# A two-layer diffusion step on one core: the modulation in 12 units of 1024 columns instead of 48 of 256

## The chip, the core and the metric

The kernel runs on one core of a Trainium2 chip. That core has TensorE (PE, with its weight loads as PEld), VectorE (DVE), ScalarE (ACT), GpSimd (POOL), SyncE (SP, which issues nearly all weight loads) and 16 DMA engines. The metric is the device time of one execution in microseconds (us), the median of three runs.

## The reference, cut to what matters

Each of two layers makes six vectors per condition from a small product, the modulation, and uses them around two halves of the layer (token mixer and expert retrieval).

```
adaLN: (shift1, scale1, gate1, shift2, scale2, gate2) = split(SiLU(cond) @ w_mod + b_mod)
h = LN(x) * (1 + scale1) + shift1        -> one projection h @ w_in, three mixers, merge
x = LN(alpha * x + gate1 * mix)
PEER (expert retrieval) on LN(x) * (1 + scale2) + shift2
x = LN(alpha * x + gate2 * ffn)
```

D_MODEL is 1024, so w_mod is 1024 x 6144 for each layer: 24 MB a layer in float32. There are two conditions only (`c_ctx` for 128 context tokens, `c` for 256 latent tokens), so the product has two rows. Its result is wanted by channel: channel on the partition, one column for each condition.

## The kernel before, in words

The 384 tokens are three tiles of 128. `mcol` holds the modulation by channel: [128 partitions, layer, part 0 to 5, 8 groups of 128 channels, 2 conditions]. Parts 0, 1 and 2 (shift1, scale1, gate1) are wanted around the mixer, 3, 4 and 5 around PEER.

A unit (`adaln_unit`) makes 256 of the 6144 columns of a layer. It loads two tiles of 512 KB (`load_k`), each with four of the eight 128-row slices of w_mod. Eight matmuls with a stationary operand of 32 columns (`condT`, two of them live) and 256 moving columns go to the four 32-wide column groups of TensorE: slice k goes to group k % 4, so four run side by side, and two are added in each group (L259). ScalarE copies the sums to `modp` (L261). Later two matmuls with the constant `sel` add the four groups and turn the result to channels (L265), and two ScalarE operations add the bias into `mcol` (L268). There are 24 units a layer, 48 in all. `adaln` begins a unit and finishes the one begun before it, so the turning of a unit stands one unit behind its product.

Where the 48 units stand: 8 in the start stage, between the transposes of the first LayerNorm (L441), for parts 0 and 1 of layer 0; 16 between the blocks of the `w_in` projection of layer 0, one after every second block (`blocks`); 4 at the entry to PEER of layer 0 and 10 in `tick`, one for each query block from the sixth on; 8 between the `w_in` blocks of layer 1 and 2 at the entry to its PEER.

A `w_in` block (`proj3`) is a load of 512 KB, a ScalarE cast to a high part (L222, `uh`), a subtraction for the low part (L224, `ul`; on GpSimd for the first three blocks, then on VectorE) and 24 matmul rows of 384 columns (L368 to L370).

Every weight load, of w_mod too, takes one of eight buffers `w` (`N_RAW`) and is issued by SP in the order written. A load waits until the buffer that it takes has been read. A scheduler chooses the order of each engine's instructions within what the data allow; PSUM buffers are rings of two to three by tag (`pp`, `pt`, `pa`; in PEER `uT` with one and `hp` with three).

The conditioning and bias are loaded by rows and turned to channels with one and two TensorE transposes (`cond_prep`).

Of the kernel before, what the change touches and what calls it, by code (L numbers as in the profile page):

```python
# [14 lines left out]
AF = mybir.ActivationFunctionType  # L15
# [22 lines left out]
N_PRE = (14, 18)  # L38
N_EXP = (10, 16)
P_TAIL = 5  # L40
N_FILL = (16, 8)
N_AD = (4, 4)
N_END = 0
N_AFF = 640
P_AFF = 512
# [5 lines left out]
N_GS = 0  # L51
U_R = {}
N_PSC = 8
R_AD = 4
CE_G = 0
S_NORM = 512
MOD_V = 1
# [50 lines left out]
    return t  # L108


CAND = []
_o = 0
for _i in range(8):
# [42 lines left out]
def hybrid_step(ctx: ExitStack, tc: tile.TileContext, A, O):  # L156
# [16 lines left out]
    def mk(p, shape, tag, dt=F32, bufs=None):  # L173
        uid[0] += 1
        kw = {} if bufs is None else {"bufs": bufs}
        return p.tile(shape, dt, name=f"{tag}_{uid[0]}", tag=tag, **kw)
# [48 lines left out]
        return hi, lo  # L225

    spool = [None]
    fill_ps, fill_n, first = [None], [0], [0]


    def cond_prep(sp, ps1):
        cond = mk(sp, [16, 128], "cond")
        dma(out=cond[0:8, :], in_=A["c_ctx"].rearrange("(k p) -> k p", p=128))
        dma(out=cond[8:16, :], in_=A["c"].rearrange("o (k p) -> (o k) p", p=128))
        V.memset(condT, 0.0)
        ps = mk(ps1, [128, 512], "pt")
        T.transpose(ps[:, :16], cond, ident[:16, :16])
        th = mk(sp, [128, 16], "cth")
        S.activation(th, ps[:, :16], AF.Tanh, scale=0.5)
        cc = mk(sp, [128, 16], "cc")  # L240
        S.activation(cc, ps[:, :16], AF.Copy, scale=0.5)
        V.scalar_tensor_tensor(condT[:, :, 0:2].rearrange("p k c -> p c k"), th.rearrange("p (c k) -> p c k", c=2), 1.0,
                               cc.rearrange("p (c k) -> p c k", c=2), op0=ALU.add, op1=ALU.mult)
        for l in range(DEPTH):
            bm = mk(sp, [48, 128], "bm", bufs=2)
            dma(out=bm, in_=A["b_mod"][l].rearrange("(k p) -> k p", p=128))
            ps = mk(ps1, [128, 512], "pt")
            T.transpose(ps[:, :48], bm, ident[:48, :48])
            V.tensor_copy(bmT[:, l], ps[:, :48])
            for part in (1, 4):  # L250
                V.tensor_scalar(bmT[:, l, part * KD:(part + 1) * KD], bmT[:, l, part * KD:(part + 1) * KD], 1.0, None, op0=ALU.add)

    def adaln_unit(l, part, hb, ps1, tags):

        w = load_k(A["w_mod"][l, part * 4 + hb])
        ps = mk(ps1, [128, 512], tags[0])
        for k in range(KD):
            q = k % 4
            T.matmul(ps[32 * q:32 * q + 32, :256], condT[:, k, :], w[k], start=(k < 4), stop=(k >= 4), tile_position=(0, 32 * q))  # L259
        mp = mk(outer, [128, 256], "modp", bufs=2)  # L260
        S.copy(mp, ps[:, :256])  # L261
        yield
        pt = mk(ps1, [128, 512], tags[1])
        for a in range(2):
            T.matmul(pt[:, 2 * a:2 * a + 2], mp[:, a * 128:(a + 1) * 128], sel, start=True, stop=True)  # L265
        c = part * KD + 2 * hb
        for a in range(2):
            S.activation(mcol[:, l, part, 2 * hb + a, :], pt[:, 2 * a:2 * a + 2], AF.Identity, bias=bmT[:, l, c + a:c + a + 1])  # L268

    todo = []  # L270
    for l, ps in ((0, (0, 1)), (0, (2,)), (0, (3, 4)), (1, (0, 1)), (0, (5,)), (1, (2,)), (1, (3, 4)), (1, (5,))):
        todo += [(l, part, hb) for hb in range(4) for part in ps]
    begun = []

    def adaln(n, ps1, tags, flush=False):

        for _ in range(min(n, len(todo))):
            u = adaln_unit(*todo.pop(0), ps1, tags)
            next(u)
            begun.append(u)  # L280
            if len(begun) > 1:
                next(begun.pop(0), None)
        while flush and begun:
            next(begun.pop(0), None)
# [88 lines left out]
    def blocks(src, b0, n):  # L373

        for j in range(n):
            yield load_w(src[b0 + j])
            if j % 2 and fill_n[0] > 0:
                fill_n[0] -= 1
                adaln(1, fill_ps[0], ("pp", "pt"))

# [37 lines left out]
    def mixer(l, stack, right, ps1):  # L418
# [4 lines left out]
        with ExitStack() as sc0:  # L423
            sp = pool(sc0, "ln")
            if l == 0:
                cond_prep(sp, ps1)
            hh = mk(mh, [128, KD, NTOK], "hh", dt=F32R)
            hl = mk(mh, [128, KD, NTOK], "hl", dt=F32R)

            if l == 0:  # L430

                xn = []
                for t in range(3):
                    xn.append(mk(sp, [128, D], "xn", bufs=3))
                    ln_norm(t, sp, xn[t])
                for k in range(KD):
                    if k % 2 == 0:
                        adaln(2, ps1, ("pp", "pt"), True)
                    ps = mk(ps1, [128, 512], "pa")
                    for t in range(3):  # L440
                        T.transpose(ps[:, t * 128:(t + 1) * 128], xn[t][:, k * 128:(k + 1) * 128], ident)  # L441
                    raw = mk(sp, [128, NTOK], "hraw", bufs=2)
                    for j, c in enumerate((slice(0, NP), slice(NP, NTOK))):
                        S.activation(raw[:, c], ps[:, c], AF.Identity, bias=mcol[:, l, 0, k, j:j + 1], scale=mcol[:, l, 1, k, j:j + 1])
                    parts(raw, hh[:, k, :], hl[:, k, :])
            for t in range(3 if l > 0 else 0):
                raw = mk(sp, [128, KD, 128], "hraw", bufs=2)
                ts = slice(t * 128, (t + 1) * 128)
                ln_mod_T(l, t, 0, 1, sp, mk(sp, [128, D], "xn", bufs=3), ps1, "pt", raw, lambda ks: parts(raw[:, ks], hh[:, ks, ts], hl[:, ks, ts], V if t == 2 else G))
        fill_ps[0], fill_n[0], first[0] = ps1, N_FILL[l], N_FIRST  # L450

        ysT = [mk(mo, [128, 4, NTOK], f"y{i}", dt=F32 if i else F32R) for i in range(3)]
        yl0 = mk(mo, [128, 4, NTOK], "ya", dt=F32R)
# [565 lines left out]
    def peer(l, mg, right, mps, ps1):  # L1019
# [161 lines left out]

        def tick(b):
            u_steps(U_R.get(b, 0))
            if l == 0 and b >= N_WQ + R_AD:
                adaln(1, pu, ("uT", "hp"), b == 15)
        later.append(tick)
        next(finding)
# [121 lines left out]
def blocked(inputs):  # L1309

    d = {k: np.asarray(v) for k, v in inputs.items()}

    def cut(w, k, n):

        m = w.shape[:-2]
        w = w.reshape(*m, -1, k, 128, w.shape[-1] // n, n)
        i = len(m)
        w = w.transpose(*range(i), i + 3, i, i + 2, i + 1, i + 4)
        return w.reshape(*m, w.shape[i], w.shape[i + 1], 128, k * n)

    wi = d.pop("w_in")
    d["w_in"] = cut(np.concatenate([wi[:, :, :1280], wi[:, :, 1296:]], axis=2), KD, 128)[:, :, 0]
    d["w_dt"] = cut(wi[:, :, 1280:1296], KD, 16)[:, 0, 0]
    d["peer_wq"] = cut(d["peer_wq"], KD, 128)[:, :, 0]
    d["w_mod"] = cut(d["w_mod"], 4, 256)
    d["w_out"] = cut(d["w_out"], 4, 256)
    d["w_branch"] = cut(d["w_branch"], 4, 256)[:, :, :, 0]
    return d
# [21 lines left out]
```

## Time and profile before

| | |
|---|---|
| median of three runs | 3023.25 us (3023.19 to 3025.1) |
| profiled execution, and its span | 3023.89 us, 3021.8 us |
| PE busy | 2880.1 us, 95% of the span |
| DVE, ACT, POOL busy | 77%, 46%, 27% |
| bytes moved | 767.09 MB, mean 254 GB/s |
| w_mod loads | 96 of 512 KB, median 4.4 us from issue to landing |
| w_in loads | 104 of 512 KB, median 3.7 us |

Stages on the clock of the trace: start (first LayerNorm, 8 units) to about 51 us; mixer of layer 0 to about 545 us; entry to PEER, query blocks and their ticks to 681 us; expert products and retrieval to about 1570 us; then layer 1 in the same order, with its entry to PEER at 2047 us.

The "PE busy" of the page counts an engine that has matmuls in its pipe. It is no measure of the array's pace: TensorE's granted clock is 2.4 GHz or 1.2 GHz, and a row of 384 columns follows the last by 0.17 or 0.32 us accordingly.

### The profile page before, as it was taken

To read this page: it belongs to the slowest core of one execution; us is meant where nothing else is said; L and a number is where in the kernel's file an instruction comes from. 1 tells how busy PE (TensorE), PEld (TensorE's weight loads), DVE (VectorE), ACT (ScalarE), POOL (GpSimd) and SP (SyncE) were. 2 spreads that over 40 slices of the span, in tenths; PEclk is the share of its full clock that TensorE was granted. 3 is DMA by queue.
4 is the path that set the end of the run, shared out by engine and by line. 5 is a ranking of instruction groups with operands and counts; after the bars stand their busy time and mean duration, and the time that the engine had idled before them with its cause. 6 is when DMAs were issued, how large, how long until landed. Compare 5 with 4: busy or idle time off the path is not lost. (4 is left out here: it accounts for less than half of the span.)

```text
span 3021.8 us, 48665 instructions
## 1 busy us (share of the span) xinstructions
PE 2880.1 (95%) x17953; PEld 2496.8 (83%) x17953; DVE 2314.3 (77%) x4888; ACT 1398.6 (46%) x2861; POOL 820.5 (27%) x566
## 2 busy tenths in 40 slices
PE   7999999999889999999969999999987999999996
PEld 5888889878779999998858888898876899999985
DVE  3745554599669999998977456446996999999988
ACT  4544542324864444444445445432168444444443
POOL 0000000101334445554530000000023444455554
PEclk9999999999999999999979999999999999999998
DMA  7445322464999999999934332124469999999994
GB/s 245 156 152 153 84 65 90 154 227 146 334 343 418 393 388 396 396 390 369 385 100 153 119 96 76 64 91 133 154 212 366 412 395 392 396 394 392 395 365 166
DMA packets 299328, 767.09 MB, mean 254 GB/s; under 512 B 42770, under 2 KB 113874, under 8 KB 299090
## 3 DMA queue, kind: packets, MB, share of 16 engines
q1 hardware_dynamic: 225362, 495.51, 46.0%
q0 software_dynamic: 73728, 268.47, 23.4%
q8 instruction: 141, 2.31, 0.3%
q14 instruction: 97, 0.79, 0.1%
HBM read 726.92 MB, written 36.96 MB: 253 GB/s over the span
## 5 line engine op out<-in xcount | busy, mean ns | idle before, releaser
L1052 POOL DMA_INDIRECT prow<-in_peer_u,ei x256 | 361.5, 1412 | 765.2 <-DVE prow L1057 521.6
L1063 POOL DMA_INDIRECT prow<-in_peer_v,ei x256 | 379.8, 1483 | 352.4 <-DVE tn L1068 310.8
L222 ACT CAST vh<-w 128x1024 fp32r<-128x1024 f32 x256 | 268.8, 1050 | 367.2 <-issue 285.6
L1162 PE MATMUL hp<-hh,uh 128*128 128x256 f32 x1488 | 433.8, 292 | 0.0
L1163 PE MATMUL hp<-hl,uh 128*128 128x256 f32 x1488 | 417.2, 280 | 0.0
L1164 PE MATMUL hp<-hh,ul 128*128 128x256 f32 x1488 | 416.8, 280 | 0.0
L1240 PE MATMUL out<-vh,al 128*128 128x512 f32 x1024 | 400.4, 393 | 3.6 <-DVE al L1225 3.6
L1239 PE MATMUL out<-vl,ah 128*128 128x512 f32 x1024 | 398.4, 391 | 3.1 <-DVE vl L224 3.1
L1238 PE MATMUL out<-vh,ah 128*128 128x512 f32 x1024 | 391.0, 398 | 1.4 <-ACT ah L1223 1.4
L224 DVE TENSOR_TENSOR vl<-w,vh 128x1024 fp32r<-128x1024 f32 x256 | 315.5, 1232 | 62.0 <-ACT vh L222 61.3
L1068 DVE SCALAR_TENSOR_TENSOR tn<-prow,pact,tn 128x1024 f32<-128x1024 f32 x254 | 325.0, 1280 | 2.7
L1150 ACT CAST uh<-w 128x1024 fp32r<-128x1024 f32 x186 | 195.4, 1051 | 251.7 <-PE hp L1163 243.0
L368 PE MATMUL pp<-hh,uh 128*128 128x384 f32 (+1 forms) x848 | 300.1, 354 | 8.9 <-ACT uh L222 4.7
L1057 DVE SCALAR_TENSOR_TENSOR prow<-prow,tn 128x1024 f32<-128x1024 f32 x256 | 302.2, 1218 | 0.3 <-DMA prow<-in_peer_u,ei 0.3
L370 PE MATMUL pp<-hh,ul 128*128 128x384 f32 (+1 forms) x848 | 296.3, 349 | 1.4 <-POOL ul L224 1.4
L1159 PE MATMUL hp<-hs,w 128*128 128x256 f32 x1120 | 266.5, 394 | 30.7 <-DMA w<-in_peer_uT 30.7
L369 PE MATMUL pp<-hl,uh 128*128 128x384 f32 (+1 forms) x848 | 295.0, 348 | 0.2 <-DVE xr L494 0.2
L1162 PEld LDWEIGHTS hp<-hh,uh 128*128 128x128 f32 x1488 | 281.3, 189 | 0.0
L1163 PEld LDWEIGHTS hp<-hl,uh 128*128 128x128 f32 x1488 | 281.2, 189 | 0.0
L1164 PEld LDWEIGHTS hp<-hh,ul 128*128 128x128 f32 x1488 | 280.4, 188 | 0.0
L1159 PEld LDWEIGHTS hp<-hs,w 128*128 128x128 f32 x1120 | 216.1, 197 | 63.0 <-DMA w<-in_peer_uT 33.5
L351 POOL TENSOR_TENSOR res<-res,lg 128x384 f32<-128x384 f32 x6 | 9.6, 1594 | 939.7 <-ACT res L313 939.7
(405 smaller groups left out, 5843.0 us busy)
## 6 DMA issues: line engine op xcount, KB each, us to landing
w<-in_peer_uT SPq DMA_DIRECT2D x256, 512.0 KB, 6.9
w<-in_peer_v SPq DMA_DIRECT2D x256, 512.0 KB, 7.2
w<-in_w_in SPq DMA_DIRECT2D x104, 512.0 KB, 3.7
w<-in_w_mod SPq DMA_DIRECT2D x96, 512.0 KB, 4.4
gd<-w SPq DMA_DIRECT2D x64, 512.0 KB, 6.1
gt<-gd SPq DMA_DIRECT2D x64, 512.0 KB, 7.4
w<-in_peer_wq SPq DMA_DIRECT2D x32, 512.0 KB, 4.4
w<-in_w_branch SPq DMA_DIRECT2D x24, 512.0 KB, 3.7
```

What stands on the lines that cost most here:

```text
L224: e.tensor_tensor(lo, src, hi.bitcast(F32), op=ALU.subtract)
L1052: G.indirect_dma_start(out=row, out_offset=None, in_=utab, in_offset=bass.IndirectOffsetOnAxis(ap=ei[:, j:j + 1], axis=0))
L1057: V.scalar_tensor_tensor(row, row, 1.0, tn, op0=ALU.mult, op1=ALU.mult, accum_out=hd[:, j:j + 1])
L1063: G.indirect_dma_start(out=row, out_offset=None, in_=vtab, in_offset=bass.IndirectOffsetOnAxis(ap=ei[:, j:j + 1], axis=0))
L1068: V.scalar_tensor_tensor(acc, row, act[:, j:j + 1], acc, op0=ALU.mult, op1=ALU.add)
L1159: T.matmul(o, ut[0][:, k, :], hs[:, k, :], start=(k == 0), stop=(k == KD - 1))
L1162: T.matmul(o, uh[:, k, :], hh[:, k, :], start=(k == 0), stop=False)
L1163: T.matmul(o, uh[:, k, :], hl[:, k, :], start=False, stop=False)
L1164: T.matmul(o, ul[:, k, :], hh[:, k, :], start=False, stop=(k == KD - 1))
L1238: T.matmul(o, ah[:, ts], vh[:, ns], start=f, stop=False)
L1239: T.matmul(o, ah[:, ts], vl[:, ns], start=False, stop=False)
L1240: T.matmul(o, al[:, ts], vh[:, ns], start=False, stop=e)
```

## The change

A unit now makes 1024 columns. The 48 units become 12 (`UNITS`: two for layer 0's shift1 and scale1, half of each in either, then one for each of the other ten parts). A unit loads eight tiles of 512 KB; tile k holds slice k of all 1024 columns. For each tile four matmuls run side by side, column group q taking 256 of the 1024 columns, and each group adds over all eight k. One ScalarE copy of 128 x 256 follows, two TensorE transposes of 128 x 128 (L262 of the changed kernel) and two VectorE additions with the bias, straight into `mcol` (four for the first two units). The bytes, the 96 loads and the 384 matmuls of w_mod are as many as before; 96 `sel` matmuls become 24 transposes, 48 copies become 12, 96 ScalarE additions become 28 on VectorE.

Where they stand: two in the start stage, five between the `w_in` blocks of layer 0 (after every sixth), one at the entry to PEER, three in the ticks of query blocks 9, 12 and 15, and the last between the blocks of layer 1. Conditioning and bias come from the host by channel, in two loads without transposes.

```diff
-N_FILL = (16, 8)
-N_AD = (4, 4)
+N_FILL = (5, 2)
+FILL_BY = 6
+N_AD = (1, 1)
...
+UNITS = [((0, 0, 0, 4), (0, 1, 0, 4)), ((0, 0, 4, 4), (0, 1, 4, 4))]
+UNITS += [((l, part, 0, 8),) for l, part in ((0, 2), (0, 3), (0, 4), (1, 0), (1, 1), (0, 5), (1, 2), (1, 3), (1, 4), (1, 5))]
...
     def cond_prep(sp, ps1):
-        cond = mk(sp, [16, 128], "cond")
-        dma(out=cond[0:8, :], in_=A["c_ctx"].rearrange("(k p) -> k p", p=128))
-        dma(out=cond[8:16, :], in_=A["c"].rearrange("o (k p) -> (o k) p", p=128))
+        cond = mk(sp, [128, 16], "cond")
+        dma(out=cond, in_=A["cond"])
+        dma(out=bmT, in_=A["b_mod"])
...
-    def adaln_unit(l, part, hb, ps1, tags):
+    def adaln_unit(u, ps1, tags):
 
-        w = load_k(A["w_mod"][l, part * 4 + hb])
         ps = mk(ps1, [128, 512], tags[0])
         for k in range(KD):
-            q = k % 4
-            T.matmul(ps[32 * q:32 * q + 32, :256], condT[:, k, :], w[k], start=(k < 4), stop=(k >= 4), tile_position=(0, 32 * q))
+            w = mk(wst, [128, RAWC], "w")
+            dma(out=w, in_=A["w_mod"][u, k])
+            for q in range(4):
+                T.matmul(ps[32 * q:32 * q + 32, :256], condT[:, k, :], w[:, q * 256:(q + 1) * 256], start=(k == 0), stop=(k == KD - 1), tile_position=(0, 32 * q))
         mp = mk(outer, [128, 256], "modp", bufs=2)
         S.copy(mp, ps[:, :256])
         yield
         pt = mk(ps1, [128, 512], tags[1])
         for a in range(2):
-            T.matmul(pt[:, 2 * a:2 * a + 2], mp[:, a * 128:(a + 1) * 128], sel, start=True, stop=True)
-        c = part * KD + 2 * hb
-        for a in range(2):
-            S.activation(mcol[:, l, part, 2 * hb + a, :], pt[:, 2 * a:2 * a + 2], AF.Identity, bias=bmT[:, l, c + a:c + a + 1])
...
+            T.transpose(pt[:, a * 128:(a + 1) * 128], mp[:, a * 128:(a + 1) * 128], ident)
+
+        pv = pt[:, :256].rearrange("p (a q m) -> p q a m", a=2, q=4)
+        j = 0
+        for l, part, k0, n in UNITS[u]:
+            for c in range(2):
+                V.tensor_tensor(mcol[:, l, part, k0:k0 + n, c].rearrange("p (q a) -> p q a", a=2), pv[:, j // 2:(j + n) // 2, :, c],
+                                bmT[:, l, part * KD + k0:part * KD + k0 + n].rearrange("p (q a) -> p q a", a=2), op=ALU.add)
+            j += n
...
-            if j % 2 and fill_n[0] > 0:
+            fill_at[0] += 1
+            if fill_n[0] > 0 and fill_at[0] % FILL_BY == 0:
...
-                    if k % 2 == 0:
-                        adaln(2, ps1, ("pp", "pt"), True)
+                    if k % 4 == 0:
+                        adaln(1, ps1, ("pp", "pt"), True)
...
-            if l == 0 and b >= N_WQ + R_AD:
+            if l == 0 and b in (9, 12, 15):
                 adaln(1, pu, ("uT", "hp"), b == 15)
```

How the instructions move is shown at three places, all on TensorE. First the start stage of the kernel before, from its third unit on (`pp` is a unit's product, `pt` its turned result, `pa` a transpose of the normalised tokens `xn`):

```order
L259 MATMUL pp_221<-w_217,condT_73 32x256 x4
L441 MATMUL pa_266<-cst_63,xn_117 128x128
L441 MATMUL pa_266<-cst_63,xn_131 128x128
L441 MATMUL pa_266<-cst_63,xn_145 128x128
L259 MATMUL pp_221<-w_219,condT_73 32x256 x4
L441 MATMUL pa_315<-cst_63,xn_117 128x128
L441 MATMUL pa_315<-cst_63,xn_131 128x128
L441 MATMUL pa_315<-cst_63,xn_145 128x128
L265 MATMUL pt_247<-cst_63,modp_230 128x2 x2
L259 MATMUL pp_236<-w_232,condT_73 32x256 x4
L259 MATMUL pp_236<-w_234,condT_73 32x256 x4
L265 MATMUL pt_252<-cst_63,modp_245 128x2 x2
```

And in the changed kernel, from the end of its second unit to the first rows of the projection (`pp_385`):

```order
L442 MATMUL pa_315<-cst_63,xn_103 128x128
L442 MATMUL pa_315<-cst_63,xn_117 128x128
L442 MATMUL pa_315<-cst_63,xn_131 128x128
L256 MATMUL pp_239<-w_264,condT_73 32x256 x4
L256 MATMUL pp_239<-w_270,condT_73 32x256 x4
L256 MATMUL pp_239<-w_276,condT_73 32x256 x4
L256 MATMUL pp_239<-w_282,condT_73 32x256 x4
L262 MATMUL pt_290<-cst_63,modp_288 128x128 x2
L368 MATMUL pp_385<-hh_101,uh_381 128x384
L369 MATMUL pp_385<-hl_102,uh_381 128x384
L442 MATMUL pa_324<-cst_63,xn_103 128x128
```

Before, product and turning alternate eight times; now there are two products with one turning behind each, and the projection's first rows follow at once, with a last transpose of tokens between them.

Second, a unit between two blocks of the layer 0 projection (`uh`, `ul` are the parts of the block's weights). Before:

```order
L369 MATMUL pp_1686<-hl_116,uh_1682 128x384
L370 MATMUL pp_1686<-hh_115,ul_1684 128x384
L259 MATMUL pp_1716<-w_1712,condT_73 32x256 x4
L259 MATMUL pp_1716<-w_1714,condT_73 32x256 x4
L265 MATMUL pt_1727<-cst_63,modp_1641 128x2 x2
L368 MATMUL pp_1738<-hh_115,uh_1734 128x384
```

And the last two of the eight rounds of the fourth unit that stands there in the changed kernel:

```order
L256 MATMUL pp_1690<-w_1727,condT_73 32x256 x4
L256 MATMUL pp_1690<-w_1733,condT_73 32x256 x4
L262 MATMUL pt_1741<-cst_63,modp_1491 128x128 x2
L748 MATMUL pa_2232<-nk_339,nq_338 128x128
L368 MATMUL pp_1753<-hh_101,uh_1749 128x384
L369 MATMUL pp_1753<-hl_102,uh_1749 128x384
```

Two rounds of four are now eight, each from a load of its own, and the next block's rows stand right behind them.

Third, the end of the ticks (L910 and L942 are a query block's products, L916 the scores `pn`, L1159 the first expert products `hp`). Before:

```order
L942 MATMUL pp_6341<-hs_4729,w_6339 128x256 x8
L259 MATMUL uT_6620<-w_6616,condT_73 32x256 x4
L259 MATMUL uT_6620<-w_6618,condT_73 32x256
L916 MATMUL pn_6358<-gel_4775,qT_6359 128x128 x3
L259 MATMUL uT_6620<-w_6618,condT_73 32x256 x3
L265 MATMUL hp_6631<-cst_63,modp_6332 128x2 x2
L265 MATMUL hp_6636<-cst_63,modp_6629 128x2 x2
L1159 MATMUL hp_6643<-hs_4729,w_5345 128x256 x8
```

And now:

```order
L943 MATMUL pp_6151<-hs_4631,w_6149 128x256 x8
L256 MATMUL uT_6426<-w_6427,condT_73 32x256 x4
L256 MATMUL uT_6426<-w_6433,condT_73 32x256
L917 MATMUL pn_6168<-gel_4677,qT_6169 128x128 x3
L256 MATMUL uT_6426<-w_6433,condT_73 32x256 x3
L256 MATMUL uT_6426<-w_6439,condT_73 32x256 x4
```

In both the scores cut one round in two; now six more whole rounds follow, and the two transposes into `hp_6482`. The bias additions that read that buffer stand far down VectorE's queue, at the end of the last query block's searches:

```order
L868 MATCH_REPLACE tktmp_1385_6402<-cv_1146_5066,cand_6352 128x50
L268 TENSOR_TENSOR mcol_72<-hp_6482,bmT_74 128x8
L869 MAX cv_1146_5066<-tktmp_1385_6402 128x8
L268 TENSOR_TENSOR mcol_72<-hp_6482,bmT_74 128x8
L870 MAX_INDEX cci_6383<-cv_1146_5066,tktmp_1385_6402 128x8
L949 TENSOR_TENSOR gt_1433_6617<-cv_1144_5064 128x128
```

They are released right ahead of the first `gt` row (L948 of the kernel before, L949 now); before, ScalarE read such a buffer. The tenth expert product after the ticks takes `hp_6482`.

## Rows read from the trace of the kernel before

**Rows 1.** PE timeline, start stage: start, duration, engine, line, operation, count, [idle<-releaser].
```profile
12.97 1.93 PE L259 MATMUL pp<-w,condT 128*32 128x256 f32 x16 [0.53 <-DVE condT L242]
...
44.58 1.01 PE L265 MATMUL pt<-cst,modp 128*128 128x2 f32 x4 [0.49 <-ACT modp L261]
49.11 0.69 PE L368 MATMUL pp<-hh,uh 128*128 128x384 f32 x1 [3.52 <-ACT uh L222]
...
51.56 0.69 PE L370 MATMUL pp<-hh,ul 128*128 128x384 f32 x1 [1.44 <-POOL ul L224]
...
56.84 0.38 PE L368 MATMUL pp<-hh,uh 128*128 128x384 f32 x1
```

**Rows 2.** Windows: length, busy time of each engine, PEclk, DMA share, GB/s.
```profile
60.00:160.00 100.00, 100.00 (x668) 82.38 (x667) 72.20 (x164) 51.23 (x128) 0.00 (x0) 1.00 0.46 152
```

**Rows 3.** PE timeline, a fill unit in the mixer of layer 0.
```profile
72.55 1.07 PE L259 MATMUL pp<-w,condT 128*32 128x256 f32 x16
73.56 0.61 PE L265 MATMUL pt<-cst,modp 128*128 128x2 f32 x4
74.02 0.43 PE L368 MATMUL pp<-hh,uh 128*128 128x384 f32 x1
```

**Rows 4.** PE timeline, entry to PEER of layer 0.
```profile
545.06 1.04 PE L329 MATMUL pa<-cst,prow 128*128 128x128 f32 x8
546.03 1.93 PE L259 MATMUL pp<-w,condT 128*32 128x256 f32 x32
547.89 0.61 PE L265 MATMUL pp<-cst,modp 128*128 128x2 f32 x4
549.78 1.07 PE L259 MATMUL pp<-w,condT 128*32 128x256 f32 x16 [1.28 <-ACT modp L261]
```

**Rows 5.** Loads issued at L210, 60 to 520 us: all landings.
```profile
DMA to landing us min/median/max: 3.3/3.7/7.3
```

**Rows 6.** DVE timeline, low part of a block's weights.
```profile
66.08 1.22 DVE L224 TENSOR_TENSOR ul<-w,uh 128x1024 fp32r<-128x1024 f32 x1
```

**Rows 7.** Costliest groups of the page: the cast of 128 x 1024.
```profile
L222 ACT CAST vh<-w 128x1024 fp32r<-128x1024 f32 x256 | 268.8, 1050 | 367.2 <-issue 285.6
```

**Rows 8.** PE timeline, the tick of one query block.
```profile
611.25 1.05 PE L259 MATMUL uT<-w,condT 128*32 128x256 f32 x10
612.23 0.94 PE L916 MATMUL pn<-gel,qT 128*128 128x128 f32 x6
613.10 0.63 PE L259 MATMUL uT<-w,condT 128*32 128x256 f32 x6
613.66 0.61 PE L265 MATMUL hp<-cst,modp 128*128 128x2 f32 x4
```

**Rows 9.** Windows over the ticks; columns as in rows 2.
```profile
650.00:660.00 10.00, 10.00 (x67) 7.96 (x67) 10.00 (x39) 1.74 (x5) 0.00 (x0) 1.00 0.44 170
```

**Rows 10.** DVE waits from 560 to 690 us: line, releaser, total, times, longest.
```profile
DVE sv L865 <- ACT psc L918: 17.9, 8, 4.0
```

**Rows 11.** DVE timeline, the last query block.
```profile
680.06 0.29 DVE L865 MAX8 sv<-psc 128x8 f32<-128x128 f32 x1 [1.36 <-ACT psc L918]
...
714.27 0.28 DVE L948 TENSOR_TENSOR gt<-cv 128x128 f32<-128x128 f32 x1
```

**Rows 12.** PE timeline after the ticks.
```profile
681.08 48.59 PE L1159 MATMUL hp<-hs,w 128*128 128x256 f32 x224
```

**Rows 13.** PE timeline, entry to PEER of layer 1.
```profile
2047.98 1.93 PE L259 MATMUL pp<-w,condT 128*32 128x256 f32 x32
...
2060.25 1.94 PE L910 MATMUL pt<-hs,w 128*128 128x128 f32 x15 [0.78 <-ACT hs L334]
```

**Rows 14.** PE timeline, rows of one column in the mixer.
```profile
183.05 2.39 PE L636 MATMUL pa<-ones,xr 128*128 128x1 f32 x20
```

**Rows 15.** Windows behind such rows, in layer 0 and layer 1.
```profile
186.00:190.00 4.00, 4.00 (x16) 3.81 (x16) 0.64 (x2) 1.59 (x2) 0.00 (x0) 0.58 0.27 110
1699.00:1705.00 6.00, 6.00 (x21) 5.23 (x21) 0.64 (x2) 1.59 (x2) 0.00 (x0) 0.50 0.20 78
```

More of the change, by code (lines that the diff above doesn't have):

```diff
@@ L227, in hybrid_step @@
     spool = [None]
-    fill_ps, fill_n, first = [None], [0], [0]
+    fill_ps, fill_n, fill_at, first = [None], [0], [0], [0]
     def cond_prep(sp, ps1):
-        cond = mk(sp, [16, 128], "cond")
-        dma(out=cond[0:8, :], in_=A["c_ctx"].rearrange("(k p) -> k p", p=128))
-        dma(out=cond[8:16, :], in_=A["c"].rearrange("o (k p) -> (o k) p", p=128))
+        cond = mk(sp, [128, 16], "cond")
+        dma(out=cond, in_=A["cond"])
+        dma(out=bmT, in_=A["b_mod"])
         V.memset(condT, 0.0)
-        ps = mk(ps1, [128, 512], "pt")
-        T.transpose(ps[:, :16], cond, ident[:16, :16])
@@ L238, in cond_prep @@
         th = mk(sp, [128, 16], "cth")
-        S.activation(th, ps[:, :16], AF.Tanh, scale=0.5)
+        S.activation(th, cond, AF.Tanh, scale=0.5)
         cc = mk(sp, [128, 16], "cc")
-        S.activation(cc, ps[:, :16], AF.Copy, scale=0.5)
+        S.activation(cc, cond, AF.Copy, scale=0.5)
         V.scalar_tensor_tensor(condT[:, :, 0:2].rearrange("p k c -> p c k"), th.rearrange("p (c k) -> p c k", c=2), 1.0,
                                cc.rearrange("p (c k) -> p c k", c=2), op0=ALU.add, op1=ALU.mult)
[L244 to L251, printed above, removed]
@@ L253, in adaln_unit @@
-    def adaln_unit(l, part, hb, ps1, tags):
-        w = load_k(A["w_mod"][l, part * 4 + hb])
+        for part in (1, 4):
+            b = bmT[:, :, part * KD:(part + 1) * KD]
+            V.tensor_scalar(b, b, 1.0, None, op0=ALU.add)
+    def adaln_unit(u, ps1, tags):
         ps = mk(ps1, [128, 512], tags[0])
         for k in range(KD):
-            q = k % 4
-            T.matmul(ps[32 * q:32 * q + 32, :256], condT[:, k, :], w[k], start=(k < 4), stop=(k >= 4), tile_position=(0, 32 * q))
+            w = mk(wst, [128, RAWC], "w")
+            dma(out=w, in_=A["w_mod"][u, k])
+            for q in range(4):
+                T.matmul(ps[32 * q:32 * q + 32, :256], condT[:, k, :], w[:, q * 256:(q + 1) * 256], start=(k == 0), stop=(k == KD - 1), tile_position=(0, 32 * q))
@@ L264, in adaln_unit @@
         for a in range(2):
-            T.matmul(pt[:, 2 * a:2 * a + 2], mp[:, a * 128:(a + 1) * 128], sel, start=True, stop=True)
-        c = part * KD + 2 * hb
-        for a in range(2):
-            S.activation(mcol[:, l, part, 2 * hb + a, :], pt[:, 2 * a:2 * a + 2], AF.Identity, bias=bmT[:, l, c + a:c + a + 1])
-    todo = []
-    for l, ps in ((0, (0, 1)), (0, (2,)), (0, (3, 4)), (1, (0, 1)), (0, (5,)), (1, (2,)), (1, (3, 4)), (1, (5,))):
-        todo += [(l, part, hb) for hb in range(4) for part in ps]
+            T.transpose(pt[:, a * 128:(a + 1) * 128], mp[:, a * 128:(a + 1) * 128], ident)
[6 more added lines that the diff above has]
+            j += n
+    todo = list(range(len(UNITS)))
     begun = []
@@ L277, in adaln @@
         for _ in range(min(n, len(todo))):
[L278 removed]
+            u = adaln_unit(todo.pop(0), ps1, tags)
             next(u)
@@ L449, in mixer @@
                 ln_mod_T(l, t, 0, 1, sp, mk(sp, [128, D], "xn", bufs=3), ps1, "pt", raw, lambda ks: parts(raw[:, ks], hh[:, ks, ts], hl[:, ks, ts], V if t == 2 else G))
-        fill_ps[0], fill_n[0], first[0] = ps1, N_FILL[l], N_FIRST
+        fill_ps[0], fill_n[0], fill_at[0], first[0] = ps1, N_FILL[l], 0, N_FIRST
         ysT = [mk(mo, [128, 4, NTOK], f"y{i}", dt=F32 if i else F32R) for i in range(3)]
@@ L1324, in blocked @@
     d["peer_wq"] = cut(d["peer_wq"], KD, 128)[:, :, 0]
-    d["w_mod"] = cut(d["w_mod"], 4, 256)
+    m = d["w_mod"].reshape(DEPTH, KD, 128, 6, KD, 128)
+    d["w_mod"] = np.stack([np.concatenate([m[l, :, :, part, k0:k0 + n].reshape(KD, 128, n * 128) for l, part, k0, n in u], axis=2) for u in UNITS])
+    d["b_mod"] = d["b_mod"].reshape(DEPTH, 48, 128).transpose(2, 0, 1)
+    d["cond"] = np.concatenate([d.pop("c_ctx").reshape(KD, 128), d.pop("c").reshape(KD, 128)]).T
     d["w_out"] = cut(d["w_out"], 4, 256)
```

1 line of the change is left out of this document (removed).

## The prediction

> **What bounds the kernel now.** I read the windows first: from 60 to 160 us, in the mixer of layer 0, TensorE is busy for 100.00 of 100 us, VectorE for 72 and the DMA engines for 0.46 [rows 2]. The timeline of TensorE then shows who is waited for at each place with units. In the mixers TensorE waits for nothing, so time taken from its queue is time won. In the start stage it works at half its pace and ends behind a chain through ScalarE and GpSimd: the last turning is at 44.58, the first row of the projection at 49.11 after 3.52 us of waiting for a cast, the first L370 at 51.56 after another 1.44 [rows 1]. At the entries to PEER it waits for a copy or for a LayerNorm [rows 4, 13]. In the ticks TensorE leads at first, since VectorE waits for scores 17.9 us in eight waits [rows 10], and later VectorE is full, 10.00 of 10 us [rows 9].
>
> **What a unit costs, before and after.** A fill unit lasts from 72.55 to 74.02: 1.01 us for two rounds of four matmuls and 0.46 for the `sel` matmuls, 1.47 in all [rows 3]. Two units back to back take 546.03 to 547.89, 1.86 for four rounds [rows 4]; so a further round adds (1.86 - 1.01) / 2 = 0.43, and entering and leaving the small form costs 0.15 a time. Eight rounds are then 1.01 + 6 x 0.43 = 3.6. A transpose of 128 x 128 is 0.97 / 8 = 0.12 [rows 4], two are 0.24. The new unit costs about 3.85; at 0.50 a round it would be 4.25, and I keep that as the dear end.
>
> The Trainium skill, "TensorEngine Tiling (Array Packing)", section Key Properties, says that changing the tiling mode drains TensorE. By that rule alone fewer entries must pay; the 0.15 of the rows agrees, and without it (0.50 a round) the total below would be 10 x 0.4 = 4 us higher.
>
> **The change part by part.**
>
> Start stage. Before, TensorE starts on the units at 12.97 and gives 0.97 to a round, half the warm pace [rows 1]. Its queue has 16 rounds, 24 transposes of tokens and 8 turnings of about 1 us [rows 1], with some 0.5 us of waiting for the copy at half of them. After, 16 rounds at 0.97 are 15.5, 24 transposes of tokens and 4 of units at twice the warm 0.12 are 28 x 0.24 = 6.7: from 12.7 to 34.9 if nothing waits. Two waits do stand there: unit 1's copy, turning and additions ahead of the first normalised tokens on ScalarE, and the rounds of unit 2 that stand behind a transpose waiting for a `pa` buffer. I give them 2 us and end the second turning at about 37.5. The first block's weights take the buffer that round 1 of unit 2 frees some 10 us earlier and land 3.7 later [rows 5], and their casts no longer stand behind the last unit, since channels 0 to 3 come from unit 1; the low part on GpSimd takes 49.11 to 51.56, 2.45 us, as before. So the first L370 comes at about 40.4, not 51.56: -11. The ends: -7, if the last transposes' tokens (channels 4 to 7, bound to unit 2) are waited for; -14, if the two waits cost nothing and the clock rises early.
>
> Fill in layer 0. Sixteen units of 1.47 are 23.5, five of 3.85 are 19.3: -4.2. But a unit now takes all eight buffers. After the first round frees one, the next block's load is issued, lands 3.7 later [rows 5], the cast takes 1.05 [rows 7], the low part 1.22 [rows 6]: 0.6 + 3.7 + 1.05 + 1.22 = 6.6 after the unit began, where TensorE is done at 3.85. The wait is 2.7 where a full block follows directly, as behind units 4 and 5; behind 3 and 6 stand other products of the mixer, and behind 2 a block of 16 columns and a queue of loads already landed. Two waits of 2.7 make +5.4, which I take as +4.7, since single products stand between; the ends are 0 (all covered) and +11 (four of the five). Sum +0.5, from -4 to +7.
>
> Entry to PEER of layer 0. Four units with their `sel` are 4 x 1.47 = 5.9, and 1.28 us of waiting for the copy stands among them [rows 4]; one unit is 3.85: -3. Ends: 0, if the loads (the same eight) set the pace there, and -4.
>
> Ticks. Here the scores cut one round in two: 0.98 + 0.56 + 0.46 = 2.0 a unit [rows 8, 3], ten are 20. After, three units of 3.85 + 0.5 for the cut round are 13: -7. Against this stand a load of the unit that takes a query block's buffer late (three times about 0.8) and VectorE. It must run 714.27 - 680.06 = 34.2 us of searches behind the last scores [rows 11], and it is full from the middle of the ticks on. The bias additions now stand in that queue, ahead of `gt`; the tenth expert product takes the buffer that they free. TensorE gets there 9 x 3.47 = 31.2 us after the ticks (48.59 / 14 = 3.47 a product [rows 12]), plus about 4 for the unit's rest behind the scores: 35, against 34.2 + 0.5. It fits with almost nothing to spare, so of 7 I take 3; the ends are 0 and -6. If VectorE is late by x, TensorE waits x.
>
> Fill in layer 1. Eight units of 1.47 are 11.8, one is 3.85: -7.9. Behind it stands the block of 16 columns: no wait; with one, -5.
>
> Entry to PEER of layer 1. Two units go, 2.8 us, but TensorE then waits for the LayerNorm 0.78 at 2060.25 [rows 13] and would wait the longer: 0, at best -2.
>
> Everything else I cost at nothing: three transposes fewer and two loads instead of four lie in front of 12.97, under the statistics of the first LayerNorm; the 28 additions on VectorE (about 0.2 each) lie in the mixers beside a TensorE that binds.
>
> Sum: -11 + 0.5 - 3 - 3 - 7.9 + 0 = -24.4. From the profiled execution's 3023.89 that is 2999.5; the median of the runs is 0.6 lower than that execution. I round to 3000.
>
> **The rivals.** *The clock falls under the long units.* Where TensorE issued rows of one column for 2.4 us [rows 14] its granted clock went to 0.58 for 4 us and, in layer 1, to 0.50 for 6 us, which is the 1.2 GHz level [rows 15]: 1.7 and 3.0 us lost each time. Ten of the new units stand in stretches at 2.4 GHz. If each is followed by a fall of 3.0 us and runs its own second half at half pace (+1.8), the price is 48 and the time 3048, slower; it tips over from 2.4 us a unit. For it: in the start stage TensorE stays at half pace for 35 us though it is rarely idle, and first speeds up at 56.84 after 5 us of full rows [rows 1]. Against it: the double units of 1.86 us, with transposes ahead, ran at full pace [rows 4, 13], and all four column groups stream 256 columns, which rows of one column don't. Chance 0.09.
>
> The Trainium skill, "TensorE: Matmul & The Clock Gate", Part 4, says that transposes don't count as work for the clock gate. No row here isolates that; by it the start stage, a third of it transposes, would stay slow as it did, and the rival needs the matmuls of units themselves to count little.
>
> *The look-ahead is lost everywhere.* One unit empties the ring of eight. If every new unit outside the start is followed by the full 2.7 us, and the ticks' gain is lost to VectorE: -11 + (19.3 - 23.5 + 5 x 2.7) + 0 + 0 - 5 = -6.7, time 3017; with the same wait at the entry to PEER (+2.7) 3020: no change. For it: the landing of 3.3 to 7.3 us [rows 5]; against it: three of the five are followed by work that needs no new weights. Chance 0.09.
>
> *More than forecast.* If the start gives 14, no fill unit is waited for (-4.2), the ticks give 6 and the entry 4: -36, time 2988. Chance 0.15.
>
> **How the numbers follow.** The forecast has 0.67; its own range, from the ends that go together, is 2988 to 3012. About 0.2% (6 us) is what a measurement of this kernel can tell from no change: 3017 to 3029. Forecast and the larger gain are all faster, and a part of the second rival: 0.84. Same 0.08, slower 0.08. The range of 8 in 10 reaches up to the second rival, 2986 to 3017.
>
> **What would show it.** In the profile after: the first L370 near 40; fill units of 8 rounds in 3.6 us and the row behind the fourth and fifth idle for 2 to 3 us on a cast or a low part of weights; no 0.50 in the granted clock behind the units in the mixers; the first expert products about 17 us earlier than 681.08; from layer 1's fill on about 24 earlier. I am wrong if the clock falls behind units, if the tenth expert product waits for VectorE by several us, or if the first L370 comes later than 45.

## The result: 19 us faster, nearly all of it in the first 35 us

The changed kernel takes 3004.31 us, median of four runs (2998.92 to 3007.38), against 3023.22 (3019.37 to 3025.1): a ratio of 0.9937, with a 95% interval of 0.9918 to 0.9956. Taken again beside the last experiments it was 3006.09 against 3023.98, ratio 0.9945 (0.9932 to 0.9959). The forecast was 3000, with a range of 2986 to 3017.

The profiled execution of the changed kernel took 3007.38 us, 16.5 less than that of before. Where the time went is read by putting the same instruction of both traces side by side. Each row below is the start of the first matmul of a line (lines of the kernel before), and "gave" is what the stretch since the row above gave. Two more columns keep single executions apart from the edit: a second profile of the changed kernel, and two profiles of the kernel before with its start alone changed (an experiment below), whose later units are the old ones.

| TensorE reaches | before | after | ahead by | the stretch gave | second profile gave | start alone gave, twice |
|---|---|---|---|---|---|---|
| first L370 of the projection | 51.6 | 35.1 | 16.4 | 16.4 | 16.8 | 16.7, 15.3 |
| out projection, L852 (mixer of layer 0 done) | 499.8 | 486.9 | 12.9 | -3.5 | -4.2 | -1.6, -0.1 |
| first L942 (entry to PEER done) | 575.3 | 557.7 | 17.6 | 4.7 | 3.1 | 4.8, 2.7 |
| first L1159 (ticks done) | 681.1 | 659.4 | 21.6 | 4.0 | 2.6 | 0.0, 0.0 |
| first L974 (index transposes) | 729.5 | 713.4 | 16.1 | -5.5 | -4.1 | 0.0, 0.0 |
| scan products of layer 1, L567 | 1611.3 | 1594.8 | 16.5 | 0.4 | -2.7 | 6.3, 1.8 |
| out projection of layer 1 | 2000.3 | 1976.4 | 23.9 | 7.4 | 7.4 | 1.6, 1.6 |
| first L942 of layer 1 | 2068.1 | 2047.9 | 20.1 | -3.8 | -2.4 | 0.0, 0.0 |
| last L1238 | 3000.1 | 2983.9 | 16.2 | -3.9 | -1.3 | -2.1, -3.4 |

Of the kernel before there is one profile, and what it had by chance stands in every row. The entry to PEER of layer 0 gave as much where the old units stand there, so its 4.7 us can't be put down to the new unit.

**The start.** TensorE's timeline of the changed kernel (start, duration, engine, line, operation, count, idle time before and what ended it), beside [rows 1]:

```profile
12.35 1.94 PE L256 MATMUL pp<-w,condT 128*32 128x256 f32 x16 [0.53 <-DVE condT L243]
...
16.90 2.75 PE L256 MATMUL pp<-w,condT 128*32 128x256 f32 x32
...
23.23 0.64 PE L256 MATMUL pp<-w,condT 128*32 128x256 f32 x8
...
27.02 1.07 PE L256 MATMUL pp<-w,condT 128*32 128x256 f32 x16
...
30.41 0.64 PE L256 MATMUL pp<-w,condT 128*32 128x256 f32 x8 [0.58 <-DMA w<-in_w_mod]
31.54 0.44 PE L262 MATMUL pt<-cst,modp 128*128 128x128 f32 x2 [0.49 <-ACT modp L258]
32.71 0.69 PE L368 MATMUL pp<-hh,uh 128*128 128x384 f32 x1 [0.73 <-ACT uh L225]
...
35.15 0.69 PE L370 MATMUL pp<-hh,ul 128*128 128x384 f32 x1 [0.72 <-POOL ul L227]
```

The first two rounds take 0.97 us each, as before. In the row of 16.90 four rounds take 2.75, and two rounds at 27.02 take 1.07 where the first two took 1.94: the pace has doubled, which it had not until 56.84 in the kernel before. At the end the rounds wait for loads of w_mod, with the DMA engines full (share 1.03 from 28 to 32 us). The half pace then comes back once: the granted clock is 0.50 from 33 to 38 us, so the first rows of the projection still go at half pace, as they did before.

**The fill units.** A unit of eight rounds lasts 3.66 us (the row of 63.58); what stands behind some of them is a wait for the next block's weights (`uh` and `ul`, its high and low part):

```profile
63.58 3.66 PE L256 MATMUL pp<-w,condT 128*32 128x256 f32 x64
...
178.11 0.44 PE L262 MATMUL pt<-cst,modp 128*128 128x128 f32 x2
...
179.75 0.45 PE L368 MATMUL pp<-hh,uh 128*128 128x384 f32 x1 [0.79 <-ACT uh L225]
...
181.01 0.44 PE L370 MATMUL pp<-hh,ul 128*128 128x384 f32 x1 [0.64 <-DVE ul L227]
```

The waits for `uh` and `ul` (lines of the changed kernel) in the mixer of layer 0, in total, times and longest:

```profile
PE pp L368 <- ACT uh L225: 3.1, 4, 1.1
PE pp L370 <- DVE ul L227: 1.9, 3, 0.6
```

After the longest of them, 1.10 and 0.64 us at 262, the granted clock fell for some 3.4 us; the window has the same columns as [rows 2]:

```profile
264.00:268.00 4.00, 4.00 (x16) 3.67 (x14) 1.95 (x5) 2.30 (x7) 0.00 (x0) 0.57 0.61 109
```

In the second profile the same wait was 1.34 and 0.64 us, and no fall followed (1.00 from 264 to 272): the fall is not a fixed price of the wait.

**The tenth expert product.** TensorE's timeline behind the ticks, beside [rows 12]:

```profile
659.44 31.25 PE L1160 MATMUL hp<-hs,w 128*128 128x256 f32 x144
694.37 19.19 PE L1160 MATMUL hp<-hs,w 128*128 128x256 f32 x80 [3.68 <-issue]
713.40 0.27 PE L975 MATMUL pp<-cst,i 128*128 128x128 f32 x1
```

Nine products (144 rows) run, and the tenth stands for 3.68 us. VectorE's timeline shows what it waited for, which the profile itself couldn't name; compare the `gt` row in [rows 11]:

```profile
694.12 0.15 DVE L268 TENSOR_TENSOR mcol<-hp,bmT 128x8 f32<-128x8 f32 x1
...
694.43 0.27 DVE L949 TENSOR_TENSOR gt<-cv 128x128 f32<-128x128 f32 x1
```

The bias addition that frees the buffer ends at 694.27, and the product starts 0.1 us later. That VectorE is late comes from the ticks: the last scores, copied by ScalarE, stand in `psc` at 655.1, and VectorE begins its search of them 5.0 us later. ScalarE's timeline, then VectorE's:

```profile
654.62 0.48 ACT L919 COPY psc<-pn 128x384 f32<-128x384 f32 x1 [1.31 <-PE pn L917]
```

```profile
660.11 0.47 DVE L866 MAX8 sv<-psc 128x8 f32<-128x128 f32 x2
```

Before, that search began as soon as the scores were there, at 680.06 [rows 11]. In the second profile it began 4.3 us behind them, and the tenth product stood for 2.22 us.

**The entry to PEER of layer 1.** No unit is left there, and TensorE now waits 3.44 us for the LayerNorm's result `prow`, with the granted clock at 0.50 behind it. Before, this wait was 0.22 us; the 0.78 us of [rows 13] is a later one, for `hs`, and stayed (0.7). TensorE's timeline, then the window behind the wait:

```profile
2034.72 1.06 PE L329 MATMUL pa<-cst,prow 128*128 128x128 f32 x8 [3.44 <-DVE prow L312]
```

```profile
2036.00:2040.00 4.00, 3.50 (x16) 3.50 (x17) 2.49 (x4) 2.52 (x7) 0.00 (x0) 0.50 0.00 0
```

### The profile page after: what moved, and what is told of

Its sections match the earlier page's. It is cut to its first block, busy times and chain, and to the rows that moved or that the text cites. A ratio compares the mean times of both kernels' runs of the same rounds, so it can differ in the third digit from the quotient of the medians.

```text
span 3005.6 us, 48181 instructions
## 1 busy us (share of the span) xinstructions
PE 2848.0 (95%) x17782; PEld 2480.0 (83%) x17782; DVE 2322.7 (77%) x4912; ACT 1370.6 (46%) x2729; POOL 820.3 (27%) x566
## 3 DMA queue, kind: packets, MB, share of 16 engines
q1 hardware_dynamic: 225490, 495.51, 45.6%
## 4 chain that ended last, share of the span: by engine, by line
PE 75%; DVE 9%; ACT 5%; DMA 5%; issue 4%; POOL 1%; SPq 0%; POOLq 0%; ACTq 0%; DVEq 0%
PE hp L1163 6%; PE hp L1164 6%; PE hp L1165 6%; PE out L1241 6%; PE out L1239 6%; PE out L1240 6%; PE hp L1160 5%; PE pp L370 4%; PE pp L368 4%; PE pp L369 4%; PE pp L943 3%; ACT ol L1000 2%; DMA w<-in_peer_uT 2%; DVE vl L227 2%; PE pp L911 2%
## 5 line engine op out<-in xcount | busy, mean ns | idle before, releaser
L1163 PE MATMUL hp<-hh,uh 128*128 128x256 f32 x1488 | 433.8, 292 | 0.0
L368 PE MATMUL pp<-hh,uh 128*128 128x384 f32 (+1 forms) x848 | 298.8, 353 | 9.7 <-ACT uh L225 5.5
L370 PE MATMUL pp<-hh,ul 128*128 128x384 f32 (+1 forms) x848 | 298.5, 352 | 2.8 <-DVE ul L227 2.1
L1163 PEld LDWEIGHTS hp<-hh,uh 128*128 128x128 f32 x1488 | 281.4, 189 | 0.0
```

The source lines that it names most:

```text
L368: T.matmul(o, wh[:, k, :], hh[:, k, :], start=(k == 0), stop=False)
L370: T.matmul(o, wl[:, k, :], hh[:, k, :], start=False, stop=(k == KD - 1))
L1163: T.matmul(o, uh[:, k, :], hh[:, k, :], start=(k == 0), stop=False)
```

## The experiments

Single runs of the kernel before, taken beside the experiments, spread from 3017 to 3033 us, so differences under some 4 us are read from the traces, not from the times.

**The start alone, and everything but the start.** The first takes the kernel before and changes only the start: two units of 1024 columns, made as in the changed kernel, then the 40 old ones. The lines that say so:

```diff
         todo += [(l, part, hb) for hb in range(4) for part in ps]
+    todo = [(0,), (1,)] + todo[8:]
...
-                    if k % 2 == 0:
-                        adaln(2, ps1, ("pp", "pt"), True)
+                    if k % 4 == 0:
+                        adaln(1, ps1, ("pp", "pt"), True)
```

> The kernel before, with two units of 1024 columns in the start stage in place of its eight of 256; all 40 later units stay as they were. Theory (the gain is made where the units stand, and the start is the largest part): the first L370 comes at 35 to 36 us and not at 51.56, of these 16 us about 14 are left at the first scan products (L528), and nothing later takes or gives: 3007 to 3010 us. Rival (what the start gains is waited for again in the mixer, where VectorE's convolution sets the pace, and the gain of the change comes from the later units): 3015 us or more.

It took 3005.13 us against 3025.28, ratio 0.9936 (0.9911 to 0.9960); the first L370 came at 34.9, and the products of L528 at 80.6, 14.0 ahead, as the theory had it; the time is 2 us below its range. The mirror image keeps the eight old units in the start of the changed kernel:

> The changed kernel with the eight units of 256 columns of the kernel before in its start stage; all ten later units have 1024. Theory: it loses 14 to 16 us against the changed kernel and ends at 3018 to 3021, so that the later units together are worth only 2 to 5 us. Rival: 3012 or less, the later units hold half of the gain or more.

3019.31, ratio 0.9986 (0.9974 to 0.9999), as the theory had it. The first L370 came at 49.8, 1.8 us ahead of the kernel before, and its first round, with the conditioning ready from the host, at 11.8 and not at 13.0. The mixer of layer 0 ended 5.7 us behind. So the start alone carries the whole measured gain; behind the old start the ten later units and the ready conditioning together are worth between nothing and 8 us.

**What holds the start at half pace.** In the changed kernel two matmuls of 128 x 2 are put behind every second round of the start:

```diff
+        few = mk(ps1, [128, 512], "pb") if u < 2 else None
...
+            if u < 2 and k % 2 == 1:
+                for a in range(2):
+                    T.matmul(few[:, 2 * a:2 * a + 2], w[:, a * 128:(a + 1) * 128], sel, start=True, stop=True)
```

> The changed kernel with two more matmuls of 128 x 2 behind every second round of the two units in the start stage, 16 in all, whose results nothing reads. Theory (in the kernel before, the turnings between the rounds are what kept TensorE at half pace through the start): rounds stay near 0.97 us through the stage, and the first L370 comes at 40 us or later instead of 35.1. Rival (half pace came from the waits between the units, not from the small matmuls): the rounds go at 0.5 from 18 us on as in the changed kernel, and the first L370 comes at 36 to 38, later by the 16 matmuls alone.

TensorE's timeline of it:

```profile
19.67 1.93 PE L257 MATMUL pp<-w,condT 128*32 128x256 f32 x16
21.53 1.01 PE L260 MATMUL pb<-cst,w 128*128 128x2 f32 x4
22.48 1.93 PE L257 MATMUL pp<-w,condT 128*32 128x256 f32 x16
...
33.50 0.61 PE L260 MATMUL pb<-cst,w 128*128 128x2 f32 x4
...
34.42 1.07 PE L257 MATMUL pp<-w,condT 128*32 128x256 f32 x16
35.42 0.61 PE L260 MATMUL pb<-cst,w 128*128 128x2 f32 x4
```

Two rounds still take 1.86 us at 19.67 and 22.48, and the pace doubles at 33 us. In all eleven profiles of kernels with the long units and no such matmuls in the start it doubles between 15.9 and 19.2. So the theory holds for the pace up to 33 us: with these matmuls between the rounds the rise comes 14 to 17 us later. They do not undo it: it came behind a stretch of rounds and transposes alone (29.94 to 32.6 us), and the last three of the eight pairs, behind it, went at full pace.

The first L370 came at 40.9, 5.8 us later. That alone would not decide: the 16 matmuls cost 8 x 0.46 = 3.7 us at full pace [rows 3] and 8 x 0.95 = 7.6 at half pace, and the waits for w_mod that they fill are gone. This kernel ran once (3014.93 us), and whether another interruption between the rounds would do the same was not tried.

**The tenth product.** ScalarE copies the transposes out of PSUM in the ticks:

```diff
+        src = pt[:, :256]
+        if tags[0] == "uT":
+            src = mk(outer, [128, 256], "modt", bufs=1)
+            S.copy(src, pt[:, :256])
...
```

> The changed kernel; in the ticks ScalarE copies the two transposes from PSUM to SBUF (128 x 256) and VectorE adds the bias from there, so that the PSUM buffer hp is free before VectorE's queue comes to the additions. Theory (the tenth expert product waits for those additions): TensorE's gap of 3.68 us at 694 is gone, the first index transposes (L975) come 4 to 5 us earlier than 713.4 and the time falls by 4 to 5, to about 3000. Rival (VectorE's searches set the way to the gathers, so TensorE only waits later): the gap moves to L975 behind VectorE's i, and the time stays at 3004.

3012.5 us, ratio 0.9959 (0.9946 to 0.9972): no gain. The gap at the tenth product was gone, but another stood in the ticks; ScalarE's timeline, then TensorE's:

```profile
652.15 0.37 ACT L267 COPY modt<-hp 128x256 f32<-128x256 f32 x1 [9.37 <-DVE mcol L272]
652.42 0.48 ACT L919 COPY qT<-pp 128x384 f32<-128x384 f32 x1
```

```profile
652.96 1.65 PE L921 MATMUL pn<-gel,qT 128*128 128x128 f32 x6 [5.45 <-ACT qT L919]
```

With a single buffer ScalarE's copy waits for VectorE's additions of the unit before, and the copy of `qT` waits behind it: VectorE's lateness had moved to another engine. The next edit avoids this: only the 16 wanted columns are copied, into one of three buffers.

> The changed kernel; in the ticks ScalarE copies only the 16 columns wanted from PSUM to SBUF, into one of three small buffers, and VectorE adds the bias from there. With one buffer (the run before) the wait at the tenth expert product was gone and 5.45 us appeared in the ticks, where ScalarE's copy waited for VectorE's additions of the unit before and the scores waited behind it. Theory: with three buffers both waits are gone, the first expert product stays near 659 us after a start like the changed kernel's, L975 comes 48 to 49 us behind it (54 in the changed kernel), and the time falls by 3 to 5. Rival (VectorE is the pace of this stretch, TensorE waits wherever it runs into it): the wait moves to L975 or the next scores and L975 comes no earlier than 713.

TensorE's timeline, beside the fence of the changed kernel above:

```profile
661.62 48.51 PE L1164 MATMUL hp<-hs,w 128*128 128x256 f32 x224
709.97 0.27 PE L979 MATMUL pp<-cst,i 128*128 128x128 f32 x1
```

All 14 products run through in 48.51 us, and the index transposes come 3.4 us before those of the changed kernel. The wait and its cause are shown; a gain in time is not: 3013.27, ratio 0.9953 (0.9936 to 0.9970). Once more:

> The changed kernel with the 16 columns copied out of PSUM, once more. Theory (the 3 to 5 us that it wins up to L975 are lost by chance in the stretch behind, which is bound by DMA): the time comes within 3 us of the changed kernel's. Rival (the copy itself costs later, whatever the profile of one run): again 6 to 9 us above the changed kernel.

3008.99, against 3006.09 for the changed kernel taken beside it: 2.9 us more, at the edge of what the theory allowed. Its index transposes stood at 708.5, and the stretch from the first index products to the first product of the experts in halves (L1009 and L1162 of the kernel before, L1010 and L1163 of the changed one) took 150.5 us, 150.1 the first time. In the changed kernel it took 145.4 and 148.0:

> The changed kernel once more, beside the next three on one chip, because its first runs were taken apart from those of the experiments. Theory (the later ten units together are worth nothing): the same time as the kernel with the start alone changed, within 2 us. Rival: 3 us or more below it. In the profile, TensorE's gap at the tenth expert product is there again, 3 to 4 us; the stretch from the first index products (L1010) to the first products of the experts in halves (L1163) took 145.4 us, and if it differs by 3 us or more this time, what the single profiles gave and took in it says nothing on the edits.

So the first products in halves come at 864.1 and 865.2 with the edit, at 863.9 and 868.5 without: what was won before the retrieval did not last through it. There the DMA engines are full (share 0.84 to 1.07 in every window of 20 us from 740 to 860, in the profiles of the changed kernel and of the three buffers) and TensorE waits for `peer_uT` and `gt`. Which transfer sets the end of that stretch was not tried. Nor is chance shown to be the cause. In the twelve profiles of kernels with long units in the start the stretch took 140.8 to 151.3 us, and the three with the 16-column copy (150.1, 150.5, and 151.3 in a run below) are the longest of them. All four runs with a copy took more time (3009 to 3013 us) than the changed kernel (3004 and 3006). So the rival, that the copy itself costs something later, stays open.

**The last unit at the entry of layer 1.** `N_FILL = (5, 2)` becomes `(5, 0)`.

> The changed kernel with its last unit at the entry to PEER of layer 1 and not between the blocks of layer 1's projection. Theory (TensorE had 3.44 us to spare there for a LayerNorm, and its clock fell after it): the unit's 3.6 us and the 1.1 us of waiting behind it go from the mixer, the gap at the entry is filled, the granted clock stays up there, and the time falls by 4 to 6, to about 2999. Rival (the unit's eight loads stand ahead of the query weights in SP's queue, and TensorE waits for these instead, as at the entry of layer 0): a wait for w from in_peer_wq of 2 to 4 us appears and the time stays within 2 us of 3004.

3004.42, ratio 0.9927 (0.9902 to 0.9952), as the changed kernel. The rival was right: out projection 27.7 us ahead of before instead of 23.9, first L942 only 20.8, since TensorE now waits for the loads. The granted clock fell all the same (0.57 on average from 2026 to 2034 us).

```profile
2024.49 0.64 PE L256 MATMUL pp<-w,condT 128*32 128x256 f32 x8 [1.02 <-DMA w<-in_w_mod]
2027.07 1.22 PE L911 MATMUL pt<-prow,w 128*128 128x128 f32 x4 [1.95 <-DMA w<-in_peer_wq]
```

**The early block.** The block behind a fill unit is loaded and split ahead of the unit:

```diff
...
+                if fill_at[0] > FILL_BY:
+                    early[b0 + j + 1] = split(load_w(src[b0 + j + 1]), spool[0], "u", 3)
                 adaln(1, fill_ps[0], ("pp", "pt"))
```

> The changed kernel; ahead of each fill unit in layer 0 but the first, the next projection block's weights are loaded, cast and split before the unit's eight loads are issued. Theory (a unit empties the ring of eight, and the block behind it waits for load, cast and low part): the waits for uh and ul behind the units at 180, 214 and 262 us (1.4, 1.2 and 1.7 us) and the fall of the granted clock at 264 are gone, the merge (L853) begins 4 to 6 us earlier, and the time falls by 4 to 6. Rival (the early block only takes the unit's place in the ring, so that the unit waits for its own last loads): waits for w from in_w_mod of the same size appear and the merge begins within 1 us of 487.

3004.3, ratio 0.9925 (0.9907 to 0.9943): nothing won. The waits at 180 and 262 were gone, those at 214 were not, and others came in their place, the longest (2.8 us) right behind the unit at 262; the waits of TensorE from 60 to 480 us:

```profile
PE pt L416 <- DVE p L413: 3.5, 5, 2.8
PE pp L369 <- ACT uh L225: 2.1, 2, 1.6
PE pt L707 <- ACT tv L704: 1.9, 1, 1.9
```

The merge came at 489.9, 3 us later than in the changed kernel. That the ring causes the waits is shown for two of the three units; how to be rid of them without others is not. Both edits together:

> Both edits together, the early block ahead of a fill unit and the 16 columns copied out of PSUM in the ticks. Theory: the two gains add, 7 to 11 us below the changed kernel, about 2995. Rival (expert retrieval further on takes its pace from the DMA engines, and what comes earlier waits there): less than 4 us.

3012.81, ratio 0.9951 (0.9934 to 0.9968): no gain added, as with the copy alone.

**Start alone again, and a mixture.**

> The kernel before with the start alone changed, once more. Theory: 3004 to 3007 us, the stretch behind the first index products between 140 and 151 us in this profile (140.8 in the first). Rival (its later stages are really faster than those of the kernel before, as the first profile had it, 25 us ahead of the kernel before at the end): 3000 or less.

3005.78, ratio 0.9946 (0.9932 to 0.9960), beside 3006.09 for the changed kernel taken with it: the same, so with the new start the ten later units are worth nothing that these times show. Its stretch behind the index products took 145.5 us, 140.8 the first time, so the 25 us lead of the first profile was partly that (17.8 this time). The mixture takes long units for the start and for eight of layer 1's ten; of its edit:

```diff
-N_FILL = (16, 8)
+N_FILL = (16, 2)
...
+UNITS = [((0, 0, 0, 4), (0, 1, 0, 4)), ((0, 0, 4, 4), (0, 1, 4, 4)), ((1, 3, 2, 6), (1, 5, 0, 2)), ((1, 4, 2, 6), (1, 5, 2, 2))]
...
+    todo = [(0,), (1,)] + todo[8:38] + [(2,), (3,)] + todo[46:]
```

> The kernel before with units of 1024 columns only where its profiles say that they pay: two in the start stage and two between the projection blocks of layer 1 (for eight of 256); the units in layer 0's projection, at both entries to PEER and in the ticks stay as before. Theory: 4 us of TensorE less in layer 1's projection and nothing lost at its entry, 2 to 4 us below the kernel with the start alone changed. Rival: the waits behind the two units take it all, the same time.

3002.5, ratio 0.9937 (0.9923 to 0.9950). It is the lowest of the three taken together, by 3.3 and 3.6 us, but the intervals overlap. Its two small units at the entry of layer 1 kept the LayerNorm's wait at 0.21 us, where the changed kernel waits 3.44.

## Why the prediction was right, step by step

The direction, the total and the place of the largest term held. Several sizes didn't, and that the total fits so well is in part luck. The start gave 5.4 us more than its -11. All that stands behind it was forecast at -13.4 and came to nothing: the lead is 16.4 us at the first L370 and 16.2 at the last L1238.

- **Start, forecast -11, measured -16.4.** Outside its own range of -7 to -14. The step that failed is "16 rounds at 0.97": only the first three to five had that price (the rise came at 17.1 and 18.6 us in the two profiles). The forecast let half pace go on to the end, and allowed the rise only in the bound. The run with small matmuls put back reached its first L370 at 40.9, beside the 40.4 of the forecast, but that nearness is chance: it carries 16 matmuls that the forecast didn't have. In one profile, of the run with the last unit at the entry of layer 1, two rounds went at half pace again (23.15 and 25.00), and the first L370 still came at 34.57: with the rise, the loads of w_mod had become the limit.
- **Fill in layer 0, forecast +0.5, measured +3.5 and +4.2.** The unit's price was exact (3.6 forecast, 3.66 measured), and so was the way to the low part (6.6 us behind the unit's start, 6.49 at 181). The waits were 5.0 us, as taken (4.7), but spread over four units, 0.6 to 1.7 each, not two of 2.7. The rest, in the first profile, is the fall of the clock behind one of them, 1.7 us, and single waits of the mixer, 0.4 to 0.8 us each. With the old units this stretch lost 0.1 and 1.6 us against the one profile of the kernel before, so 2 to 4 us are the new units'.
- **Entry to PEER of layer 0, forecast -3, measured -4.7 and -3.1.** Near in size, but not shown to come from the unit: with the old units it gave 4.8 and 2.7. The waiting for the copy went as forecast (1.3 us), and waits for loads came for it (0.9 for w_mod; 1.8 for the query weights, 1.2 before). What differs most between the profiles is the clock: 0.50 from 552 to 560 us in the kernel before, 0.60 from 540 to 544 in the changed one, 1.00 from 530 to 575 in one profile with the old units. That was not priced.
- **Ticks, forecast -3, measured -4.0 and then +5.5 (second profile -2.6 and +4.1).** "If VectorE is late by x, TensorE waits x" is what happened, at the buffer named, with 3.68 and 2.22 us. The step that failed is the start of VectorE's searches: the forecast let them begin with the last scores, and they began 5.0 us behind them. The ticks were shorter for TensorE and VectorE, already full, didn't follow. Behind the wait the clock fell as well: 0.72 on average from 693 to 699, 1.7 us.
- **Fill in layer 1, forecast -7.9, measured -6.8.** From the layer's first L368 to its out projection TensorE took 433.6 us instead of 440.4. The 7.4 of the table is what left behind L567, five units of 1.47; three more had stood ahead of it, where the new unit now stands with a wait of 1.1 us behind it. The forecast had no wait there.
- **Entry of layer 1, forecast 0, measured +3.8 and +2.4.** A wait for the LayerNorm took the place of the units, as said, but for its result and not for the `hs` of [rows 13]; that TensorE would fall to 1.2 GHz for it was not forecast.
- **What the forecast left out.** A stretch bound by DMA differs by 3 to 5 us between two executions of one kernel. The forecast moved a lead as if it would last to the end.

Two readings in the prediction are off without changing this. Transposes are not a third of the start: from 12.97 to 45.6 us they take 5.5. And of the way from 34.9 to 40.4 it names 2 and 2.45 us; the last 1.05 has no row.

Of the rivals, the fall of the clock *under* the units didn't happen: where eight rounds ran unbroken they took 3.66 us, at full pace. Where it fell and had not before (264, 693 and 2036 us), TensorE had just waited 1.7 to 3.7 us, though one wait of 2.0 us, in the second profile, was followed by no fall. What makes the clock fall stays open. By the prediction's reading of the Trainium skill, "TensorE: Matmul & The Clock Gate", Part 4, the start would have stayed slow for its transposes; with as many transposes of tokens as before the pace doubled at 18.6 us. So the transposes alone don't hold the start at half pace; whether they count is not shown, since no run takes them out. The lost look-ahead happened in part: it turned the fill of layer 0 from a forecast gain of 4 to a loss of 3.5.

## What to carry to other kernels

Fewer and longer units brought a gain that lasted in one place only, where TensorE was the chain, ran at half pace and was interrupted by tiny matmuls. Elsewhere they gained and lost the same again. Where the same work was filler between blocks, its short pieces had filled waits for loads and for a LayerNorm, and long pieces cost a ring of buffers its look-ahead. Before a result moves to another engine's queue, look at how late that queue is and which PSUM buffer the result holds meanwhile. And take a second profile before a stretch of some us is put down to an edit.

## What the runs showed of the hardware

- With pairs of two-column matmuls between the rounds of the start, the half pace lasted to 33 us in one profile; with long units and no such pairs it ended between 15.9 and 19.2 us in eleven. Three pairs behind the rise went at full pace.
- The column of the granted clock shows 1.00 where the rounds prove half pace, from 12 to 17 us of the changed kernel. Its first record is the rise at 18.6, so the column says nothing of the time ahead of it:

```profile
12.00:17.00 5.00, 4.65 (x34) 1.91 (x38) 2.51 (x11) 2.56 (x5) 0.00 (x0) 1.00 1.03 419
```

- A stretch of retrieval with full DMA engines took 140.8 and 145.5 us in two executions of one kernel, and 145.4 and 148.0 in two of another. A single profile says nothing of 5 us there.
